# Where the 32 gate columns of the input projection are multiplied: from a fifth product of the first stage to a tail on the moving operand of the first value projection

## The chip, the core and the metric

The kernel runs on one core of a Trainium2 chip, as one program. The metric is the device time of one execution in microseconds (us); lower is better. The core's engines are named as in the profile: PE is TensorE's matrix multiplier, PEld its weight load (the stationary operand, which overlaps the multiplications), DVE is VectorE, ACT is ScalarE, POOL is GpSimd and SP is SyncE, which here only issues transfers. Each engine works through its own list of instructions in a fixed order; semaphores join the lists.

## What is computed

One layer of a decoder: a normalized input is projected to many groups of columns, two kinds of attention run on them, and an output projection and a SwiGLU feed-forward follow. For 512 tokens and a model width of 2048, the part that matters here is the combined input projection:

```python
h = _rms_norm(x, attn_norm[l])
proj = h @ w_in
qf, kf, vf, ff, qn, kc, vc, ks, vs, kw, vw, gt = jnp.split(proj, cuts, axis=-1)
log_f = jax.nn.log_sigmoid(ff + fox_forget_bias)         # 8 columns: forget gates
cum_f = jnp.transpose(jnp.cumsum(log_f, axis=1), (0, 2, 1))
gates = jax.nn.sigmoid(gt).reshape(B, T, G, R, 3)        # 24 columns: branch gates
```

`ff` (8 columns) and `gt` (24 columns) are the 32 gate columns. `kc` and `vc` (256 columns each) feed the compressed branch, `vs` and `vw` are values of the selected and of the window branch, two heads of 128 columns each, `ks`, `kw` and `qn` are keys and queries. The gates are first needed when the first attention head scales its probabilities, and the cumulative forget gate much later.

## The kernel before

**Precision.** All products are formed from operands split in two parts: `hi`, the value rounded to the fast format by an ACT copy, and `lo`, the rest, by a DVE subtraction. A product takes three matmuls: hi·hi, hi·lo and lo·hi (`mm3`, lines 170 to 173).

**First stage (lines 654 to 684).** A loop over the 16 blocks `k` of 128 input columns loads a block of x (`xs`, 256 KB) and of the weights of kc and vc (`ws`, 256 KB), splits x times its norm gain into `bigm` (kept for the whole attention part as the list `xg`) and the weights into `w0p`, and accumulates four products `first[0..3]`, one 128-column group each, all 512 tokens as moving operand. The row norm of x is not applied yet; squares of x are summed in `acc` on the side, and `rstd`, the reciprocal root, is multiplied in afterwards. `first[4]` is the fifth product: the 32 gate columns. Their weights `wf` (hi and lo side by side, 64 columns for each `k`) are stationary, and the hi and the lo part of x move through: two matmuls for each `k`, lines 675 to 677, into one PSUM bank of tag "o". The weights arrive in one transfer of 256 KB (`ws_fg`) at `k == 0` and are split by one ACT and one DVE instruction (lines 670, 671).

**Buffers.** `w0p`, `wf` and later all split projection weights are tiles of the tag "wp", of which there are two; raw weights are tiles "ws" (three) or "ox" (sixteen). A tile has to be released by its last reader before the next user of its slot can write. PSUM has eight banks, by tags: "g" two, "s" two, "t" two, "o" one, "m" one.

**After the first stage.** `ks0` is projected with the weights stationary (48 matmuls of 512 columns, lines 171 to 173), the row norm is finished meanwhile (`row_rstd`), and `unload` evicts `first[0..3]` times `rstd` as `t_kc` and `t_vc` (line 312) and `first[4]` as `fg` (line 698). It also transposes `rstd` into `rcol`, one column for each block of 128 tokens (line 703). Then `values(("vs0", "vw0"))` projects the values of both branches for the first head with the **tokens stationary**: for each chunk `c` of four `k`, each half `b` of the tokens, each `kk`, each block `t` of 128 tokens, three matmuls whose moving operand is 256 weight columns. Two banks "g" hold the four token blocks, two blocks each. The evictions (line 377 through `split2`) multiply by `rcol`.

**The gates.** `gates` (line 554) transposes `fg` back to tokens on partitions with four matmuls (line 558), adds the hi and lo halves to `tf`, and goes on to the branch gates `gate` and the cumulative sum (`lf`, `lfr`, a triangular product `ps_cum`).

**Order.** The program text interleaves a main list of steps with a side list (`weave`); after that a scheduler orders each engine's list before the run, so what stands where on an engine follows from its estimate of what is ready. The main list here is `values`, then the projections kw0, qn0 and qn1; the side list is the rest of `unload`, then `windows` and `compress` of kc (matmuls `z_kc`), `gates`, and the same for vc.

Of the kernel before, what the change touches and what calls it, by code (L numbers as in the profile page):

```python
# [17 lines left out]
P = 128  # L18
# [52 lines left out]
def hybrid_layer(ctx: ExitStack, tc: tile.TileContext, xT, vec, ffb, wfg, wfirst, win, cmpw, wout, wgu, wdn, out):  # L71
# [55 lines left out]
    def ftile(name):  # L127
        return pers.tile([P, T], F32, tag="f", name=name, bufs=4)
# [12 lines left out]
    def cut(m, at, n):  # L141
        return m[:, at:at + n]
# [11 lines left out]
    def parts_tile(name):  # L154
        return wpl.tile([P, 2 * HALF * P + P], FR, tag="wp", name=name, bufs=2)
# [138 lines left out]
    def gain(i):  # L294
        return gains[:, i:i + 1]
# [4 lines left out]
    rows = ap_.tile([P, 64], FR, name="rows")  # L300
    nc.vector.tensor_tensor(rows, rowsf, rowsf[:, 31:32].to_broadcast([P, 64]), op=OP.add)
    rcol = ap_.tile([P, NB], F32, name="rcol")


    nproj = [0]
# [46 lines left out]
        split2(r, t)  # L352
        live[name] = r

    def values(pair):

        z = [ps.tile([P, T], F32, tag="g", name=f"ps_{pair[0]}{b}", bufs=2) for b in range(2)]
        i = nproj[0]
        nproj[0] += 2
        for c in range(4):  # L360
            wp = load_w(win[i + c // 2, c % 2], f"{pair[0]}_{c}", 1 if c else 2)
            for b in range(2):
                for kk in range(4):
                    x = xg[4 * c + kk]
                    ws = slice(kk * 2 * HD, (kk + 1) * 2 * HD)
                    for t in range(2):
                        at = slice((2 * b + t) * P, (2 * b + t + 1) * P)
                        for n, (xp, w) in enumerate(((0, 0), (0, 1), (1, 0))):
                            nc.tensor.matmul(z[b][:, t * 2 * HD:(t + 1) * 2 * HD], x[:, xp, at], wp[w][:, ws],  # L369
                                             start=(c == 0 and kk == 0 and t == 0 and n == 0),  # L370
                                             stop=(c == 3 and kk == 3 and n == 2), skip_group_check=True)
                    yield
                if c == 3:
                    r = ap_.tile([P, 2, T], FR, tag="kv", name=f"{pair[0]}{b}", bufs=5)
                    for t in range(2):
                        ts = slice(t * 2 * HD, (t + 1) * 2 * HD)
                        split2([r[:, p, ts] for p in range(2)], z[b][:, ts], rcol[:, 2 * b + t:2 * b + t + 1])
                    live[pair[0], b] = r
        for n, name in enumerate(pair):
            def part(p, j, n=n, r=[live[pair[0], b] for b in range(2)]):  # L380
                return cut(r[j // 2][:, p], (2 * (j % 2) + n) * HD, HD)
            live[name] = part
# [170 lines left out]

    def gates():

        tp = ps.tile([P, NB, 64], F32, tag="t", name="ps_fgT", bufs=2)
        for i in range(NB):
            nc.tensor.transpose(tp[:, i, :], tokens["fg"][:64, i * P:(i + 1) * P], ident[:64, :64])
        yield
        tf = ftile("tf")[:, :NB * 32].rearrange("p (i c) -> p i c", c=32)  # L560
        nc.scalar.activation(tf, tp[:, :, :32], AF.Copy)
        nc.vector.tensor_tensor(tf, tf, tp[:, :, 32:], op=OP.add)
# [87 lines left out]
    for _ in range(WARM):  # L650
# [1 line left out]


    first = [ps.tile([P, T], F32, tag=tag, name=f"ps_first{i}", bufs=n)
             for i, (tag, n) in enumerate((("s", 2), ("s", 2), ("t", 2), ("t", 2), ("o", 1)))]
    for k in range(NK):
        xs = oxp.tile([P, T], F32, tag="ox", name=f"x_{k}", bufs=16)
        nc.sync.dma_start(xs, xT[k])
        ws = oxp.tile([P, T], F32, tag="ox", name=f"w0_{k}", bufs=16)
        nc.sync.dma_start(ws, wfirst[k])  # L660
        t = big(k)
        split(t, xs, v1(V_AN + k))
        wp = parts_tile(f"w0p_{k}")[:, :2 * T].rearrange("p (s c) -> p s c", s=2)
        w_done = split(wp, ws)
        if k == 0:
            wst = wpl.tile([P, HALF * P], F32, tag="ws", name="ws_fg", bufs=3)[:, :NK * 32]
            nc.sync.dma_start(wst, wfg)
            wst = wst.rearrange("p (k c) -> p k c", c=32)
            wf = parts_tile("wf")[:, :NK * 64].rearrange("p (k s c) -> p k s c", k=NK, s=2)
            nc.scalar.activation(wf[:, :, 0], wst, AF.Copy)  # L670
            nc.vector.tensor_tensor(wf[:, :, 1], wst, wf[:, :, 0].bitcast(F32), op=OP.subtract)
        for j in range(4):
            c = slice(j * P, (j + 1) * P)
            mm3(first[j], wp[:, 0, c], wp[:, 1, c], t[:, 0], t[:, 1], k == 0, k == NK - 1)
        for hl in range(2):
            nc.tensor.matmul(first[4][:64], wf[:, k], t[:, hl], start=(k == 0 and hl == 0),
                             stop=(k == NK - 1 and hl == 1))
        if k == 0:
            tc.add_manual_dep(nc.scalar.activation(acc, xs, AF.Square).ins, w_done.ins.name, PACE)
        else:  # L680
            sq = ftile(f"sq{k}")
            nc.scalar.activation(sq, xs, AF.Square)
            nc.vector.tensor_tensor(acc, acc, sq, op=OP.add)
        xg.append(t)


    ks0 = normed("ks0", gain(V_SK), "kv", 5)
    next(ks0)
    row_rstd("r1")

    def unload():
        for j, which in enumerate(("kc", "vc")):
            tokens[which] = []
            for g in range(2):
                tokens[which].append(scaled(first[2 * j + g], f"{which}{g}", True))
                yield
        fg = oxp.tile([P, T], F32, tag="ox", name="fg", bufs=16)
        nc.vector.tensor_tensor(fg[:64], first[4][:64], rstd[:64], op=OP.mult)
        tokens["fg"] = fg
        yield  # L700
        tr = ps.tile([P, NB, NH], F32, tag="t", name="ps_rT", bufs=2)
        for i in range(NB):
            nc.tensor.transpose(tr[:, i, :], rstd[:NH, i * P:(i + 1) * P], ident[:NH, :NH])
        nc.vector.tensor_copy(rcol, tr[:, :, 0])
        yield
# [1 line left out]
    N, NS, F, FS = 18, 26, 53, 12  # L707
    tokens_out = unload()
    weave(ks0, itertools.islice(tokens_out, 2), N, 2, 11)
    weave(stagger(values(("vs0", "vw0")), normed("kw0", gain(V_WK), "kv"), nsa_q(0), nsa_q(1)),  # L710
          chain(tokens_out, windows("kc", V_PK), compress("kc"), gates(), windows("vc", V_PV), compress("vc")), 5 * NK, 52, 10)
    def qf(h):
        return normed(f"qf{h}", gain(V_FQ), "q", 2)

# [602 lines left out]
```

## Time and profile before

| | |
|---|---|
| time, median of 3 runs (lowest to highest) | 2114.24 us (2113.95 to 2114.70) |
| the profiled execution: its time, its span | 2114.38 us, 2112.6 us |
| granted TensorE clock, mean | 1.00 |
| matmuls / DVE / ACT instructions in the span | 15675 / 2458 / 1242 |
| first stage, first to last matmul | 5.88 to 57.63 us of the span |
| `ks0` projection | 57.63 to 68.98 us |
| values of vs0 and vw0 | 68.98 to 96.18 us |

The span runs from the first to the last instruction of the profiled execution, and 1.8 us of its time lie around it. In a view of groups, a row has the line, the engine, the operation, the tile written and the tiles read, the shapes, the count, and then the busy time. In a timeline the first two columns are the start and the duration in us, and brackets at the end give the idle time of the engine before this row and what ended it. In a view of windows the columns are the length of the window and then, for each engine, the busy time with the count of instructions, the granted clock, the share of the DMA engines and GB/s. Durations of matmuls overlap (one is still draining when the next has begun), so the cost of one is the distance from start to start, not its duration.

### The profile page before, as it was taken

What the parts mean: (1) busy time and instruction counts of PE and PEld (TensorE: products, weight loads), DVE (VectorE), ACT (ScalarE), POOL (GpSimd) and SP (SyncE); (2) the same over time, 40 slices, a digit from 0 to 9 for tenths busy, and PEclk for the clock granted to TensorE, in tenths of its full rate; (3) what the DMA queues carried; (4) which work ended last, traced back from release to release, by engine and by line L of the source; (5) the groups of instructions that cost most, each with busy time, mean ns of one, the idle gap of its engine ahead of it and who ended that gap; (6) DMA issues with size and microseconds to landing.
All of it is one profiled execution on the core that took longest, in us unless ns stands there. A gap on an engine that the chain in (4) does not pass through costs nothing.

```text
span 2112.6 us, 37997 instructions
## 1 busy us (share of the span) xinstructions
PE 2101.6 (99%) x15675; PEld 1974.6 (93%) x15675; DVE 1675.4 (79%) x2458; ACT 999.7 (47%) x1242; POOL 190.7 (9%) x283
## 2 busy tenths in 40 slices
PE   9999999999999999999999999999999999999999
PEld 7878988888988888999999999999999999999999
DVE  6667667554567454999999999899999987889898
ACT  5555555444455343544334343343343455565554
POOL 0000000111211000111111111111111000000000
PEclk9999999999999999999999999999999999999999
DMA  5422111222222444676776777777787798579865
GB/s 196 160 75 62 61 58 58 65 86 85 90 85 75 152 137 137 170 188 202 193 195 189 193 197 182 201 187 184 205 191 195 225 335 270 151 233 329 302 174 149
DMA packets 113486, 349.63 MB, mean 165 GB/s; under 512 B 13592, under 2 KB 13592, under 8 KB 113312
## 3 DMA queue, kind: packets, MB, share of 16 engines
q1 hardware_dynamic: 85552, 270.33, 39.5%
q0 software_dynamic: 22144, 52.44, 14.0%
q10 hardware_dynamic: 5616, 24.43, 2.9%
q8 instruction: 122, 2.00, 0.4%
q14 instruction: 52, 0.43, 0.1%
HBM read 318.56 MB, written 74.73 MB: 186 GB/s over the span
## 4 chain that ended last, share of the span: by engine, by line
PE 85%; issue 9%; DVE 3%; POOL 1%; ACT 1%; DMA 0%; POOLq 0%; SPq 0%; ACTq 0%; DVEq 0%
PE q L1067 39%; PE pd L1206 13%; PE pd L1211 6%; PE po L172 3%; PE po L173 3%; PE po L171 3%; PE ps_vs L369 2%; PE ps_vf L369 1%; PE ps_qn L171 1%; PE ps_qn L173 1%; PE ps_qn L172 1%; POOL nbf L628 1%; PE ps_first L171 1%; PE ps_first L173 1%; PE ps_first L172 1%
## 5 line engine op out<-in xcount | busy, mean ns | idle before, releaser
L82 ACT ACTIVATE bigm<-r 128x1792 fp32r<-128x1792 f32 x174 | 298.2, 1714 | 461.1 <-PE q L1067 263.4
L79 DVE TENSOR_TENSOR bigm<-r,bigm 128x1792 fp32r<-128x1792 f32 x174 | 351.5, 2020 | 13.2 <-ACT bigm L82 12.7
L79 DVE TENSOR_TENSOR r<-r 128x512 f32<-128x512 f32 x522 | 267.2, 512 | 27.5 <-DMA r<-wgu 15.2
L1067 PE MATMUL q<-bigm 128*128 128x256 f32 x1848 | 217.5, 276 | 0.2 <-ACT bigm L82 0.2
L1067 PE MATMUL q<-formy,bigm 128*128 128x256 f32 x1848 | 217.1, 276 | 0.0
L1067 PE MATMUL q<-forma,bigm 128*128 128x256 f32 x1848 | 216.8, 276 | 0.0
L1067 PE MATMUL q<-formx,bigm 128*128 128x256 f32 x1848 | 216.8, 276 | 0.0
L1067 PEld LDWEIGHTS q<-bigm 128*128 128x128 f32 x1848 | 213.3, 188 | 0.6 <-ACT bigm L82 0.4
L1067 PEld LDWEIGHTS q<-formy,bigm 128*128 128x128 f32 x1848 | 213.1, 188 | 0.1
L1067 PEld LDWEIGHTS q<-forma,bigm 128*128 128x128 f32 x1848 | 213.0, 188 | 0.1
L1067 PEld LDWEIGHTS q<-formx,bigm 128*128 128x128 f32 x1848 | 212.9, 188 | 0.0
L124 POOL DMA_DIRECT2D wsum<-wdn x176 | 119.8, 687 | 878.7 <-ACT bigm L82 773.7
L1206 PE MATMUL pd<-bigm 128*128 128x256 f32 x1200 | 146.9, 276 | 0.0
L1206 PEld LDWEIGHTS pd<-bigm 128*128 128x128 f32 x1200 | 141.0, 188 | 0.0
L79 DVE TENSOR_TENSOR bigm<-wd,bigm 128x1024 fp32r<-128x1024 f32 (+1 forms) x62 | 107.8, 1739 | 12.3 <-ACT bigm L82 12.2
L82 ACT ACTIVATE bigm<-rawm 128x768 fp32r<-128x768 f32 (+2 forms) x72 | 66.0, 927 | 98.2 <-PE pd L1211 63.8
L369 PE MATMUL ps_vf<-wp_vf,bigm 128*128 128x256 f32 x768 | 101.7, 282 | 0.0
L171 PE MATMUL po<-bigm,wp_o 128*128 128x512 f32 x256 | 99.7, 389 | 0.0
L172 PE MATMUL po<-bigm,wp_o 128*128 128x512 f32 x256 | 99.7, 389 | 0.0
L173 PE MATMUL po<-bigm,wp_o 128*128 128x512 f32 x256 | 99.6, 389 | 0.0
L369 PEld LDWEIGHTS ps_vf<-wp_vf,bigm 128*128 128x128 f32 x768 | 95.1, 189 | 1.5 <-issue 0.7
L82 ACT ACTIVATE bigm<-wd 128x1024 fp32r<-128x1024 f32 (+1 forms) x62 | 91.1, 1469 | 10.7 <-DVE wd L79 6.1
(479 smaller groups left out, 3975.8 us busy)
## 6 DMA issues: line engine op xcount, KB each, us to landing
r<-wgu SPq DMA_DIRECT2D x174, 512.0 KB, 4.3
wsum<-wdn POOLq DMA_DIRECT2D x176, 256.0 KB, 5.1
rawm<-ad SPq DMA_DIRECT2D x44, 512.0 KB, 6.9
wd<-wdn SPq DMA_DIRECT2D x40, 512.0 KB, 6.0
wd<-wsum SPq DMA_DIRECT2D x40, 512.0 KB, 7.0
ad<-cb ACTq DMA_DIRECT2D x22, 896.0 KB, 6.0
rawm<-ad SPq DMA_DIRECT2D x44, 384.0 KB, 3.8
ws_o<-wout SPq DMA_DIRECT2D x28, 512.0 KB, 3.6
```

The costliest lines, as they stand in the source:

```text
L79: return pin(nc.vector.tensor_tensor(*args, op=op))
L82: return pin(nc.scalar.activation(*args, **kw))
L124: d = nc.gpsimd.dma_start(step[0], step[1], **step[2])
L171: nc.tensor.matmul(o, lh, rh, start=start, stop=False)
L172: nc.tensor.matmul(o, lh, rl, start=False, stop=False)
L173: nc.tensor.matmul(o, ll, rh, start=False, stop=stop)
L369: nc.tensor.matmul(z[b][:, t * 2 * HD:(t + 1) * 2 * HD], x[:, xp, at], wp[w][:, ws], start=(c == 0 and kk == 0 and t == 0 and n == 0), sto ...
L628: nc.gpsimd.tensor_scalar(nb[:, :n], ck[:, :n], ncq[:, i, h:h + 1], 1.0, op0=OP.add, op1=OP.mult)
L1067: nc.tensor.matmul(o, w[wp][:, fb, cs], a[:, xp, fa], start=(k == 0 and h == 0 and wp == 0 and xp == 0), stop=(g == NG - 1 and kk == 1 and ...
L1206: nc.tensor.matmul(b[q][k][:, h * 256:(h + 1) * 256], w[0][:, fb, q * P:(q + 1) * P], a[xp][:, fa], start=(j == 0 and h == 0 and xp == 0), ...
L1211: nc.tensor.matmul(b[q][k][:, h * 256:(h + 1) * 256], w[1][:, fb, q * P:(q + 1) * P], a[0][:, fa], start=False, stop=(j == NJ - 1), skip_g ...
```

## The change

The fifth product of the first stage goes, with its bank, its weight tile `wf`, the load `ws_fg` at `k == 0`, the split of the weights, the eviction `fg` and the four transposes in `gates`. The same 256 KB of gate weights are loaded once after the first stage as `gcols`. `values(("vs0", "vw0"), gcols)` appends them to the moving operand: the hi tile of a chunk has for each `k` 256 value columns, 32 gate columns hi and 32 gate columns lo. The three matmuls of a token block become x hi times 320 columns, x hi times 256 columns (the lo part of the value weights, now in two tiles of the sixteen "ox" buffers), and x lo times 288 columns. A block of 128 tokens now fills 320 columns, so each has a bank of its own: "g", "o", "s", "g". At the end one ACT and one DVE instruction for each block put the gate columns, times `rcol`, into `tf`. All other value projections are as before; the side list has two steps fewer, so its stated length falls from 52 to 50.

```diff
-    def values(pair):
+    def values(pair, gcols=None):
...
+            z = [ps.tile([P, T], F32, tag=tag, name=f"ps_{pair[0]}{t}", bufs=n)
+                 for t, (tag, n) in enumerate((("g", 2), ("o", 1), ("s", 2), ("g", 2)))]
...
+                st = wpl.tile([P, HALF * P], F32, tag="ws", name=f"ws_{name}", bufs=3)
+                load(st, w)
+                st = st.rearrange("p (k c) -> p k c", k=4)
+                hi = cut(parts_tile(f"wp_{name}"), VOFF, 4 * 320).rearrange("p (k c) -> p k c", k=4)
+                nc.scalar.activation(hi[:, :, :256], st, AF.Copy)
+                g = gcols[:, 4 * c:4 * c + 4]
+                nc.scalar.activation(hi[:, :, 256:288], g, AF.Copy)
+                lo = []
+                for n in range(2):
+                    t = loose(f"wl_{name}{n}").rearrange("p (k c) -> p k c", k=2)
+                    nc.vector.tensor_tensor(t, st[:, 2 * n:2 * n + 2], hi[:, 2 * n:2 * n + 2, :256].bitcast(F32), op=OP.subtract)
+                    lo += [t[:, kk] for kk in range(2)]
+                nc.vector.tensor_tensor(hi[:, :, 288:320], g, hi[:, :, 256:288].bitcast(F32), op=OP.subtract)
+                wp = [[hi[:, kk, :320] for kk in range(4)], lo, [hi[:, kk, :288] for kk in range(4)]]
+                cols = [320, 256, 288]
...
-                        for n, (xp, w) in enumerate(((0, 0), (0, 1), (1, 0))):
-                            nc.tensor.matmul(z[b][:, t * 2 * HD:(t + 1) * 2 * HD], x[:, xp, at], wp[w][:, ws],
+                        for n, xp in enumerate((0, 0, 1)):
+                            nc.tensor.matmul(z[2 * b + t][:, :cols[n]], x[:, xp, at], wp[n][kk],
...
+        if gcols is not None:
+            for t in range(NB):
+                rc = rcol[:, t:t + 1]
+                nc.scalar.activation(tf[:, t], z[t][:, 288:320], AF.Copy, scale=rc)
+                nc.vector.scalar_tensor_tensor(tf[:, t], z[t][:, 256:288], rc, tf[:, t], op0=OP.mult, op1=OP.add)
...
     def gates():
-        tp = ps.tile([P, NB, 64], F32, tag="t", name="ps_fgT", bufs=2)
-        for i in range(NB):
-            nc.tensor.transpose(tp[:, i, :], tokens["fg"][:64, i * P:(i + 1) * P], ident[:64, :64])
-        yield
-        tf = ftile("tf")[:, :NB * 32].rearrange("p (i c) -> p i c", c=32)
-        nc.scalar.activation(tf, tp[:, :, :32], AF.Copy)
-        nc.vector.tensor_tensor(tf, tf, tp[:, :, 32:], op=OP.add)
...
-             for i, (tag, n) in enumerate((("s", 2), ("s", 2), ("t", 2), ("t", 2), ("o", 1)))]
+             for i, (tag, n) in enumerate((("s", 2), ("s", 2), ("t", 2), ("t", 2)))]
...
-        if k == 0:
-            wst = wpl.tile([P, HALF * P], F32, tag="ws", name="ws_fg", bufs=3)[:, :NK * 32]
-            nc.sync.dma_start(wst, wfg)
-            wst = wst.rearrange("p (k c) -> p k c", c=32)
-            wf = parts_tile("wf")[:, :NK * 64].rearrange("p (k s c) -> p k s c", k=NK, s=2)
-            nc.scalar.activation(wf[:, :, 0], wst, AF.Copy)
-            nc.vector.tensor_tensor(wf[:, :, 1], wst, wf[:, :, 0].bitcast(F32), op=OP.subtract)
...
-        for hl in range(2):
-            nc.tensor.matmul(first[4][:64], wf[:, k], t[:, hl], start=(k == 0 and hl == 0),
-                             stop=(k == NK - 1 and hl == 1))
...
+    gcols = oxp.tile([P, T], F32, tag="ox", name="gcols", bufs=16).rearrange("p (k c) -> p k c", c=32)
+    nc.sync.dma_start(gcols.rearrange("p k c -> p (k c)"), wfg)
...
-        fg = oxp.tile([P, T], F32, tag="ox", name="fg", bufs=16)
-        nc.vector.tensor_tensor(fg[:64], first[4][:64], rstd[:64], op=OP.mult)
...
-    weave(stagger(values(("vs0", "vw0")), normed("kw0", gain(V_WK), "kv"), nsa_q(0), nsa_q(1)),
-          chain(tokens_out, windows("kc", V_PK), compress("kc"), gates(), windows("vc", V_PV), compress("vc")), 5 * NK, 52, 10)
+    weave(stagger(values(("vs0", "vw0"), gcols), normed("kw0", gain(V_WK), "kv"), nsa_q(0), nsa_q(1)),
+          chain(tokens_out, windows("kc", V_PK), compress("kc"), gates(), windows("vc", V_PV), compress("vc")), 5 * NK, 50, 10)
```

More of the change, by code (lines that the diff above doesn't have):

```diff
@@ L302, in hybrid_layer @@
     rcol = ap_.tile([P, NB], F32, name="rcol")
+    tf = ap_.tile([P, NB, 32], F32, name="tf")
     nproj = [0]
@@ L353, in normed @@
         live[name] = r
-    def values(pair):
-        z = [ps.tile([P, T], F32, tag="g", name=f"ps_{pair[0]}{b}", bufs=2) for b in range(2)]
+    def values(pair, gcols=None):
+        if gcols is None:
+            z = [ps.tile([P, T], F32, tag="g", name=f"ps_{pair[0]}{b}", bufs=2) for b in range(2)]
+            z = [z[t // 2][:, t % 2 * 2 * HD:(t % 2 + 1) * 2 * HD] for t in range(NB)]
+        else:
+            z = [ps.tile([P, T], F32, tag=tag, name=f"ps_{pair[0]}{t}", bufs=n)
+                 for t, (tag, n) in enumerate((("g", 2), ("o", 1), ("s", 2), ("g", 2)))]
         i = nproj[0]
@@ L360, in values @@
         for c in range(4):
-            wp = load_w(win[i + c // 2, c % 2], f"{pair[0]}_{c}", 1 if c else 2)
+            name = f"{pair[0]}_{c}"
+            w = win[i + c // 2, c % 2]
+            if gcols is None:
+                wp = [[x[:, kk * 2 * HD:(kk + 1) * 2 * HD] for kk in range(4)] for x in load_w(w, name, 1 if c else 2)]
+                wp.append(wp[0])
+                cols = [2 * HD] * 3
+            else:
+                st = wpl.tile([P, HALF * P], F32, tag="ws", name=f"ws_{name}", bufs=3)
[13 more added lines that the diff above has]
+                cols = [320, 256, 288]
             for b in range(2):
@@ L364, in values @@
                     x = xg[4 * c + kk]
-                    ws = slice(kk * 2 * HD, (kk + 1) * 2 * HD)
                     for t in range(2):
                         at = slice((2 * b + t) * P, (2 * b + t + 1) * P)
-                        for n, (xp, w) in enumerate(((0, 0), (0, 1), (1, 0))):
-                            nc.tensor.matmul(z[b][:, t * 2 * HD:(t + 1) * 2 * HD], x[:, xp, at], wp[w][:, ws],
-                                             start=(c == 0 and kk == 0 and t == 0 and n == 0),
+                        for n, xp in enumerate((0, 0, 1)):
+                            nc.tensor.matmul(z[2 * b + t][:, :cols[n]], x[:, xp, at], wp[n][kk],
+                                             start=(c == 0 and kk == 0 and n == 0 and (t == 0 or gcols is not None)),
                                              stop=(c == 3 and kk == 3 and n == 2), skip_group_check=True)
@@ L376, in values @@
                         ts = slice(t * 2 * HD, (t + 1) * 2 * HD)
-                        split2([r[:, p, ts] for p in range(2)], z[b][:, ts], rcol[:, 2 * b + t:2 * b + t + 1])
+                        split2([r[:, p, ts] for p in range(2)], z[2 * b + t][:, :2 * HD], rcol[:, 2 * b + t:2 * b + t + 1])
                     live[pair[0], b] = r
+        if gcols is not None:
[3 more added lines that the diff above has]
+                nc.vector.scalar_tensor_tensor(tf[:, t], z[t][:, 256:288], rc, tf[:, t], op0=OP.mult, op1=OP.add)
         for n, name in enumerate(pair):
@@ L696, in unload @@
                 yield
-        fg = oxp.tile([P, T], F32, tag="ox", name="fg", bufs=16)
-        nc.vector.tensor_tensor(fg[:64], first[4][:64], rstd[:64], op=OP.mult)
-        tokens["fg"] = fg
-        yield
         tr = ps.tile([P, NB, NH], F32, tag="t", name="ps_rT", bufs=2)
```

## The prediction

> **What bounds the kernel now.** I read the busy times and the chain of waits first.
>
> ```profile
> PE 2101.6 (99%) x15675; PEld 1974.6 (93%) x15675; DVE 1675.4 (79%) x2458; ACT 999.7 (47%) x1242; POOL 190.7 (9%) x283
> PE 85%; issue 9%; DVE 3%; POOL 1%; ACT 1%; DMA 0%; POOLq 0%; SPq 0%; ACTq 0%; DVEq 0%
> ```
>
> PE is busy from end to end, so time is gained or lost where PE's own list grows or shrinks, or where PE waits. Next I cut the stages that the change touches into windows: all engines, then the matmuls into `ps_first` alone, before and after the last gate matmul, and DVE's load while x is being split.
>
> ```profile
> 5.88:57.63 51.75, 51.75 (x225) 39.96 (x225) 33.02 (x55) 29.67 (x51) 0.83 (x1) 1.00 0.49 178
> 57.63:68.98 11.35, 11.35 (x51) 9.38 (x50) 9.16 (x11) 6.01 (x9) 0.00 (x0) 1.00 0.45 140
> 68.98:96.18 27.20, 26.14 (x218) 25.50 (x216) 14.08 (x23) 13.15 (x22) 0.00 (x0) 1.00 0.70 232
> ...
> 5.88:33.10 27.22, 27.22 (x116) 19.69 (x117) 0.00 (x0) 1.00 0.93 337
> 33.10:57.63 24.53, 24.53 (x109) 20.08 (x107) 0.00 (x0) 1.00 0.00 1
> ...
> 5.25:33.10 27.85, 27.50 (x117) 19.69 (x117) 26.42 (x46) 24.13 (x43) 0.83 (x1) 1.00 0.93 337
> ```
>
> The first stage has no PE idle time. The second part holds 108 matmuls (the 109th starts the next stage): 24.53/108 = 227 ns each, for 512 columns. The first part, where DVE is 95% busy and the gate matmuls run, takes 27.22/116 = 235 ns each. The granted clock is 1.00 throughout.
>
> **Removed from the first stage.** These rows show the gate matmuls, and how ACT's writes of `w0p` wait for PE.
>
> ```profile
> L676 PE MATMUL ps_first<-bigm,wf x32: 387/390/398, 8.7 to 32.9; 128*64 128x512 f32 x32
> ...
> 6.12 0.64 ACT L670 ACTIVATE wf<-ws_fg 128x512 fp32r<-128x512 f32 x1 [0.30 <-DMA ws_fg<-wfg]
> 16.77 0.63 ACT L82 ACTIVATE w0p<-w 128x512 fp32r<-128x512 f32 x1 [0.38 <-PE ps_first L173]
> 36.07 0.63 ACT L82 ACTIVATE w0p<-w 128x512 fp32r<-128x512 f32 x1 [2.13 <-PE ps_first L173]
> ```
>
> The stage keeps 192 matmuls. If the 84 early ones keep 235 ns and 108 have 227 ns, it lasts 44.2 us, 7.5 less; if all have 227 ns, 43.6 us, 8.15 less. There is one trap. While `wf` holds one of the two "wp" slots, `w0p` has the other alone: ACT may write block k only when PE has finished block k-1 (16.77), and the four or five gate matmuls, about 1.1 us, are what PE does during that 0.63 us copy. They look like filler. But the slot leaves with them. After the last gate matmul both slots serve `w0p`: ACT waits 2.13 us for PE (36.07), is a block ahead, and PE has no gap. In the changed kernel's order ACT writes the second `w0p` directly after the second x, and the load of `wfg`, third in SP's queue, is replaced there by x, so each early load lands one place earlier. DVE is the tight one; its three steps for a block follow each other here:
>
> ```profile
> 13.89 0.69 DVE L79 TENSOR_TENSOR w0p<-w,w0p 128x512 fp32r<-128x512 f32 x1
> 14.50 0.69 DVE L683 TENSOR_TENSOR acc<-acc,sq 128x512 f32<-128x512 f32 x1
> 15.10 0.74 DVE L138 SCALAR_TENSOR_TENSOR bigm<-x,vt,bigm 128x512 fp32r<-128x512 f32 x1
> 15.76 0.69 DVE L683 TENSOR_TENSOR acc<-acc,sq 128x512 f32<-128x512 f32 x1
> ```
>
> From start to start they take 0.61, 0.60 and 0.66 us. Its new order puts all sixteen splits of x and sums and eleven `w0p` first: 16 x 1.26 + 11 x 0.61 = 26.9 us from 5.25, done at 32.2 with nothing idle; PE asks for the eleventh `w0p` at its 123rd matmul, 5.88 + 122 x 0.23 = 33.9. So DVE keeps ahead by a microsecond or so, and small steps in between take part of it. I take **-7.7**, bounds -8.15 and -6.0 (1.5 us lost to DVE).
>
> **Removed with the transposes.** Four transposes, and a slow re-entry of the next matmul.
>
> ```profile
> 109.44 0.41 PE L558 MATMUL ps_fgT<-ident,fg 64*128 64x64 f32 x4
> 109.78 0.50 PE L171 MATMUL ps_kw<-bigm,wp_kw 128*128 128x512 f32 x1
> 110.11 0.40 PE L172 MATMUL ps_kw<-bigm,wp_kw 128*128 128x512 f32 x1
> ```
>
> 109.78 - 109.44 = 0.34 us. The re-entry (0.33 instead of 0.23) probably stays with the transpose `zkT` ahead of it. **-0.35**, bounds -0.45 and -0.3.
>
> **Added columns.** Of the 192 value matmuls, 64 grow by 64 and 64 by 32 columns. The trace has no such lengths; the nearest rows are a window of 256-column matmuls and the value matmuls themselves.
>
> ```profile
> 1000.00:1100.00 100.00, 100.00 (x885) 1.00 0.73 188
> ...
> 73.59 7.77 PE L369 MATMUL ps_vs<-wp_vs,bigm 128*128 128x256 f32 x66
> 81.29 0.41 PE L703 MATMUL ps_rT<-ident,rstd 8*128 8x8 f32 x4
> ```
>
> 100/885 = 113 ns for 256 columns, 227 for 512: (227 - 113)/256 = 0.446 ns a column, so 64 x (64 + 32) x 0.446 = **+2.74**. In place the 66 value matmuls take 7.70/66 = 117 ns, so 192 of them carry 0.7 us over the dense pace. Longer matmuls may absorb that (low bound +2.0); the lo part at another place in memory, and the 320-column stride, may double it, and a bit (high bound +4.0). I stay with 2.74.
>
> The Trainium skill (TensorE: Matmul & The Clock Gate, Back-to-back issue gap) gives columns/2.4 + 2.5 ns when warm: 109 and 216 ns, where the rows have 113 and 227. By its slope the added columns would be an estimated 2.56 us instead of 2.74; the rows decide.
>
> **The wait in front of `ss_ks`.** The only PE wait of this stage, and the ACT and DVE rows that lead to it:
>
> ```profile
> 72.53 0.50 PE L259 MATMUL ss_ks<-fr_ks,ones 128*128 128x512 f32 x1 [1.01 <-ACT fr_ks L82]
> ...
> 69.15 1.19 ACT L472 ACTIVATE xb_kc<-qq 128x480 fp32r<-128x480 f32 x2 [2.07 <-DVE qq L473]
> 70.25 1.05 ACT L82 ACTIVATE wp_vs<-ws_vs 128x1024 fp32r<-128x1024 f32 x1
> 71.20 0.61 ACT L334 ACTIVATE sq_ks<-t_ks 128x512 f32<-128x512 f32 x1
> 71.84 0.63 ACT L82 ACTIVATE fr_ks<-sq_ks 128x512 fp32r<-128x512 f32 x1
> ...
> 64.77 2.12 DVE L312 TENSOR_TENSOR t_vc<-ps_first,rstd 128x512 f32<-128x512 f32 x2
> 67.87 0.67 DVE L698 TENSOR_TENSOR fg<-ps_first,rstd 64x512 f32<-64x512 f32 x1
> 69.83 0.67 DVE L314 TENSOR_TENSOR t_ks<-ps_ks,rstd 128x512 f32<-128x512 f32 x1
> ```
>
> ACT idled 2.07 us for DVE, which was evicting `t_vc` (2.12). In the new order `t_vc` stands behind `fr_ks`, and `fg` is gone. On the old clock `t_ks` can then start at about 69.2, the second weight copy when its slot is free (69.1, 1.05 us), the square at 70.2, a small gate copy, `fr_ks` hi at 71.0 to 71.5. PE reaches `ss_ks` after 19 matmuls, six triples of 142 + 113 + 127 ns and one more: 68.98 + 2.44 = 71.4. About 0.2 us are left of 1.01: **-0.8**, bounds -1.1 and 0.
>
> **Preparation, evictions, loads: hidden.**
>
> ```profile
> L82 ACT ACTIVATE vs<-ps_vs,rcol x8: 456/474/477, 92.3 to 267.3; 128x256 fp32r<-128x256 f32 x8
> L151 DVE SCALAR_TENSOR_TENSOR vs<-ps_vs,rcol,vs x8: 455/479/483, 92.8 to 268.4; 128x256 fp32r<-128x256 f32 x8
> L561 ACT ACTIVATE tf<-ps_fgT x1: 278/278/278, 109.9 to 109.9; 128x128 f32<-128x128 f32 x1
> L562 DVE TENSOR_TENSOR tf<-tf,ps_fgT x1: 286/286/286, 110.2 to 110.2; 128x128 f32<-128x128 f32 x1
> 66.73 1.22 DVE L79 TENSOR_TENSOR wp_vs<-ws_vs,wp_vs 128x1024 fp32r<-128x1024 f32 x1
> 85.98 0.40 PE L489 MATMUL z_kc<-wp_kc,qq 128*128 128x256 f32 x2
> 96.18 0.39 PE L171 MATMUL ps_kw<-bigm,wp_kw 128*128 128x512 f32 x1
> ```
>
> A chunk's split grows from two to five instructions: one more on ACT (under 0.28 us, the 128-wide row) and on DVE two halves of 0.69 and a small one for one of 1.22, some 0.45 us more. The first was ready 1.0 us before PE's 68.98; with `t_vc` out of its way it is ready earlier still. The `tf` reads are eight instructions of under 0.29 us. The one PE could wait for is block 0's: its bank goes to `kw0` next. Blocks 0 and 1 end 24 matmuls (3 us) and three `z_kc` pairs before `kw0`, the two copies, two `wp_kc` splits and two `tf` reads ahead of that take about 3.0 us, so it is covered with under 1 us to spare; uncovered, it would cost up to 2. On SP, `gcols` stands behind the last load of x, far from its use. Two weight loads have moved ahead of the first `kc` loads, and the second waits for the raw tile of chunk 1, free at about 71.4 of the old clock; `z_kc` starts at 85.98, late enough. In `gates`, `zkT` now stands after the triangle's first matmul, and DVE writes that triangle between the small steps of `zks`: some 0.2 us. With 0.3 for DVE in the first stage: **+0.5**, bounds 0 and 1.5. Behind 150 us the instructions stand in the old order on every engine, so what is gained by then stays.
>
> **Sum.** -7.7 - 0.35 + 2.74 - 0.8 + 0.5 = -5.6. The profiled execution took 2114.38 (span 2112.6), the median of the runs is 0.14 less: 2114.38 - 5.6 - 0.14 = **2108.6 us**.
>
> **Rivals.**
> *The filler was needed.* Should `w0p` keep one slot for the first eight blocks, PE would stand still for each copy instead of doing gate matmuls, the 7.7 are not gained, and the added columns stay: 2114.24 - 0.35 + 2.74 = 2116.6, slower. The price decides against the change once the gaps exceed the forecast's 5.6 us over the seven blocks, 0.8 each. For it: 16.77. Against it: 36.07 and the new order.
> *DVE becomes the bound of the first stage.* At 95% busy, and with PE now asking every 2.73 us instead of 3.9, PE could wait 0.5 us at each of six blocks: 3 us, 2111.6. For it: the 26.42 of 27.85 us. Against it: a removed 0.69 us split, and DVE's second half of the stage nearly empty.
> *A new wait in the values:* `kw0` behind block 0's `tf`, or a late chunk: +2 us, 2110.6. For it: under 1 us to spare.
> *Alternating banks slow PE.* The four blocks are now written in turn to separate banks. Should the granted clock fall to half for the values, 24 us of matmuls double: about 2132. Against it: the first stage changes its bank among five all the time and its rows show clock 1.00.
> The Trainium skill (TensorE: Matmul & The Clock Gate, A second HAM failure mode: psum-queue depth-cycling) describes a kernel that cycled PSUM banks, idled briefly between groups and oscillated between the two clocks; the trace here disagrees, with 1.00 in that stage.
>
> **How the numbers follow.** Forecast 0.72; DVE bound 0.10; new wait 0.10; filler 0.06; banks 0.02. The forecast's own terms, all at their low bounds, give 2106.5, and all at their high bounds 2112; the first two rivals that follow lie inside. The range is 2106.4 to 2112.0. A measurement of this kernel can tell 0.2%, 4.2 us: below 2110.0 is faster. The forecast reaches over that in one case of ten (0.07); DVE's bound (0.10) and half of the new wait (0.05) lie within 0.2%, the other half below; filler and banks are slower: faster 0.70, same 0.22, slower 0.08.
>
> **What would show it.** The last `ps_first` matmul some 7.7 us earlier and no ACT, DVE or DMA named before `ps_first` matmuls; value triples of 383 ns; the `ss_ks` wait under 0.4 us; no idle time before the first `ps_kw`; the order and pace unchanged behind 150 us. Idle time in front of `ps_first`, or a value pace far over 383 ns a triple, would prove it wrong.

## The result, and the profile after

The changed kernel takes 2111.25 us (median of 20 runs, 2110.48 to 2111.92), the kernel before 2114.48 in the same comparison (20 runs, 2113.74 to 2115.24): a ratio of 0.9984, 95% interval 0.9979 to 0.9990, so some 3.2 us less. The forecast was 5.6 less, 2108.6 us; the time lies inside the range, but 2.65 us above the forecast.

The page of the changed kernel says the same of the bound as before, its busy times and its chain of waits:

```profile
PE 2095.5 (99%) x15639; PEld 1973.3 (94%) x15639; DVE 1674.8 (79%) x2467; ACT 1000.0 (47%) x1248; POOL 191.8 (9%) x283
PE 86%; issue 9%; DVE 2%; POOL 1%; ACT 1%; DMA 0%; POOLq 0%; SPq 0%; ACTq 0%; DVEq 0%
```

PE has 36 matmuls less, the 32 of the gates and the four transposes. To see where the time went, the span is cut at the first matmuls of the stages, the same ones in both kernels. The windows of the changed kernel (columns: start and end, length, then busy time and instructions of PE, PE's weight loads, DVE, ACT, POOL; granted clock, DMA share, GB/s; the fourth stretch of the table is left out) are: first stage; the `ks` projection; the values up to the first `ps_kw`; the attention and the output projection; the first 336 matmuls of the feed-forward stage; the rest.

```profile
5.88:49.56 43.68, 43.68 (x192) 36.15 (x193) 31.89 (x54) 28.24 (x50) 2.04 (x1) 1.00 0.56 207
49.56:60.91 11.35, 11.35 (x51) 9.38 (x50) 8.01 (x13) 7.25 (x12) 0.00 (x0) 1.00 0.38 114
60.91:89.96 29.05, 29.05 (x218) 28.36 (x217) 17.25 (x31) 13.91 (x27) 0.00 (x0) 1.00 0.59 196
...
167.92:841.09 673.17, 670.32 (x3693) 575.35 (x3691) 401.57 (x796) 324.40 (x579) 50.32 (x70) 1.00 0.27 88
...
841.09:884.23 43.14, 40.01 (x337) 39.13 (x336) 35.97 (x51) 20.22 (x20) 5.48 (x8) 1.00 0.60 162
...
884.23:2108.90 1224.67, 1220.04 (x10758) 1219.84 (x10756) 1124.00 (x1399) 558.86 (x468) 129.17 (x191) 1.00 0.73 212
```

The windows of the kernel before for the last three (its first three stand in the prediction: 51.75, 11.35 and 27.20):

```profile
174.76:847.88 673.12, 670.31 (x3692) 575.31 (x3691) 400.60 (x796) 324.50 (x579) 50.22 (x70) 1.00 0.28 89
...
847.88:887.84 39.96, 39.76 (x338) 39.23 (x336) 36.98 (x52) 20.22 (x20) 5.55 (x9) 1.00 0.64 168
...
887.84:2112.50 1224.66, 1220.03 (x10758) 1219.83 (x10756) 1124.50 (x1399) 558.22 (x468) 129.16 (x191) 1.00 0.75 212
```

| stretch | before | after | difference |
|---|---|---|---|
| first stage | 51.75 | 43.68 | -8.07 |
| `ks` projection | 11.35 | 11.35 | 0 |
| values, to the first `ps_kw` | 27.20 | 29.05 | +1.85 |
| from there to 174.76 (before) and 167.92 (after) | 78.58 | 77.96 | -0.62 |
| attention and output projection | 673.12 | 673.17 | +0.05 |
| first 336 matmuls of the feed-forward stage | 39.96 | 43.14 | **+3.18** |
| the rest | 1224.66 | 1224.67 | 0 |

The sum is -3.61, the difference of the spans (2109.0 and 2112.6). So the change as such brought 6.84 us up to 170 us, more than the forecast's 5.6, and PE kept them for 670 us. Then, in one place, 3.2 were given back. The timeline of the changed kernel there:

```profile
841.09 5.11 PE L1080 MATMUL q<-forma,bigm 128*128 128x256 f32 x42
841.28 0.33 SPq L85 DMA_DIRECT2D cb<-wgu  x1
...
844.99 1.61 DVE L79 TENSOR_TENSOR cb<-cb 128x512 f32<-128x512 f32 x3 [4.45 <-DMA cb<-wgu]
...
846.68 1.70 ACT L82 ACTIVATE bigm<-cb 128x1792 fp32r<-128x1792 f32 x1 [8.55 <-DVE cb L79]
...
848.43 5.15 PE L1080 MATMUL q<-formx,bigm 128*128 128x256 f32 x42 [2.24 <-ACT bigm L82]
```

And of the kernel before:

```profile
839.55 0.33 SPq L85 DMA_DIRECT2D r<-wgu  x1
842.63 0.33 SPq L85 DMA_DIRECT2D cb<-wgu  x1
...
847.88 5.11 PE L1067 MATMUL q<-forma,bigm 128*128 128x256 f32 x42
```

`cb` takes the second block of weights of the feed-forward stage. Before, its load went out 5.25 us ahead of the first `q` matmul; after, 0.19 us behind it. It lands 3.6 us later, DVE makes three sums of it, ACT copies it, and PE, done with the first 42 matmuls, stands still for 2.24 us, and for 0.59 and 0.15 us in front of two later groups. The waits of SP's queue name the releaser (total, times, longest). In the changed kernel and in the one before:

```profile
SPq L85 <- PE po L173: 8.5, 1, 8.5
```

```profile
SPq L85 <- PE po L173: 2.7, 1, 2.7
```

In both kernels the load waits for PE's matmuls of the output projection. How long the row is says little, since it counts from when the queue comes to this load (in e5 below it reads 8.1 us, and the load is in time). What counts is which matmul releases it. The 5.25 us ahead of the first `q` matmul and the 0.19 us behind it lie 5.44 us apart, which is 24 matmuls of 227 ns, PE's work on one `wp_o` tile. So the load now waits for one `wp_o` tile more than before. Nothing of the change touches that load, and SP's list of instructions is the same there. What has changed is where things lie. When the output projection ends, the pool of the weight ring closes, and the feed-forward stage's tiles are laid into the same memory:

```python
    wst_.close()
    fpl = ctx.enter_context(tc.tile_pool(name="fpl", bufs=1, side="right", reuse_waits="tile"))
    ca = fpl.tile([P, 4, T], F32, name="ca")
    cb = fpl.tile([P, 4, T], F32, name="cb")
```

The addresses that the two programs give to these tiles when they are built (bytes in a partition), with what the slot held last:

| memory | before | after | laid over it |
|---|---|---|---|
| "wp" slot A, 199200 to 207904 | last `wp_o` | last but one | `ca` (200224 to 208416) |
| "wp" slot B, 207904 to 216608 | last but one | **last `wp_o`** | **`cb`** (208416 to 216608) |
| "ws" slots 2 and 3, 220704 to 228896 | last raw `ws_o` (slot 3) | last but one (slot 2) | `r0` |

With `wf` gone from the two slots, the later tiles of the ring come to lie one slot further, down to the last weights of the output projection. That was theory S: `cb` now lies over the last `wp_o`, so its load must wait for PE's last matmul of the projection. The rivals: the loads of the new stage can't come 6.8 us earlier whatever the slot (T), or something that the earlier order of work has moved.

### The profile page after: what moved, and what is told of

It is laid out like the page before. It is cut to its first block, busy times and chain, and to the rows that moved or that the text cites. A ratio compares the mean times of both kernels' runs of the same rounds, so it can differ in the third digit from the quotient of the medians.

```text
span 2109.0 us, 37948 instructions
## 1 busy us (share of the span) xinstructions
PE 2095.5 (99%) x15639; PEld 1973.3 (94%) x15639; DVE 1674.8 (79%) x2467; ACT 1000.0 (47%) x1248; POOL 191.8 (9%) x283
## 4 chain that ended last, share of the span: by engine, by line
PE 86%; issue 9%; DVE 2%; POOL 1%; ACT 1%; DMA 0%; POOLq 0%; SPq 0%; ACTq 0%; DVEq 0%
PE q L1080 39%; PE pd L1219 13%; PE pd L1224 6%; PE po L172 3%; PE po L173 3%; PE po L171 3%; PE ps_vs L396 2%; PE ps_vf L396 1%; PE ps_qn L171 1%; PE ps_qn L173 1%; PE ps_qn L172 1%; POOL nbf L653 1%; PE ps_first L171 1%; PE ps_first L173 1%; PE ps_first L172 1%
```

## The experiments

The times of the kernel before beside these runs were 2114.3 (e1 to e4), 2114.52 (e5 to e7) and 2114.43 us (e8, e9); ratios are to it.

**e1: the ring turned by one.** In front of the first stage:

```diff
+    shift = parts_tile("shift")
+    nc.gpsimd.memset(shift[:, :32].bitcast(F32), 0.0)
     for k in range(NK):
```

> The changed kernel with one more tile in the ring of two weight slots: before the first stage a tile of the "wp" ring is taken and 32 of its columns are set to zero by POOL, so the first w0p takes the other slot, and so does every tile behind it; the last wp_o lies where it lay before the change. Nothing else is changed. Theory S (the slot): the changed kernel is 6.8 us ahead up to the last output projection (828 us of the old trace) and gives 3.2 back at the start of the feed-forward stage, because the tile cb lies over the slot that now holds the last wp_o, so its load waits for PE's last po matmul. Then here the load of cb is issued about 5 us before the first q matmul again, the waits of 2.2 and 0.6 us in front of q are gone, and the time is 2111.25 - 3.2 = 2108.05 (2107.7 to 2108.5). Rival T (the loads of the feed-forward stage cannot come 6.8 us earlier, whatever slot cb has: queue, transfers, the ring of raw tiles that is also turned by one): the waits stay, 2111.2. Rival E (the turned order of the first splits costs the first stage something): between the two.

Measured: 2112.88 us, 0.9993 (0.9984 to 1.0002), far from 2108.05. The timeline of its start and its windows (first stage; first 336 matmuls of the feed-forward stage) show two things:

```profile
9.42 0.61 ACT L699 ACTIVATE sq<-x 128x512 f32<-128x512 f32 x1
...
9.94 1.13 ACT L82 ACTIVATE w0p<-w 128x512 fp32r<-128x512 f32 x2
...
10.61 0.79 PE L171 MATMUL ps_first<-bigm,w0p 128*128 128x512 f32 x1 [5.46 <-ACT w0p L82]
```

```profile
10.61:56.23 45.62, 45.62 (x192) 37.50 (x193) 29.50 (x45) 25.74 (x44) 0.21 (x1) 0.95 0.46 159
847.64:886.58 38.94, 38.94 (x337) 38.87 (x336) 35.50 (x51) 20.36 (x21) 5.49 (x8) 1.00 0.62 168
```

The added tile had moved the first `w0p` behind four splits of x and a square on ACT; PE stood still for 5.46 us and then ran at a lower granted clock (0.95 over the stage), so the first stage ended at 56.23 instead of 49.56. But the feed-forward stage's first 336 matmuls took 38.94 instead of 43.14 us, with no wait: 4.2 us less, against an expected 3.2. The slot theory held at its place; the repair had spoilt another one. Rival E, a cost in the first stage, had been given at most the 3.2 us that S gains; at 6.67 us it was larger than the gain.

**e2: `ca` and `cb` exchanged in the kernel before.**

```diff
-    ca = fpl.tile([P, 4, T], F32, name="ca")
     cb = fpl.tile([P, 4, T], F32, name="cb")
+    ca = fpl.tile([P, 4, T], F32, name="ca")
```

> The kernel before with the allocations of ca and cb in the other order, so that cb lies over the slot that holds the last wp_o and ca over the other; the first 600 us are untouched, and no work comes earlier or later up to there. Theory S: the load of cb is issued right behind PE's last po matmul (848 instead of 842.6 us), PE waits 2 to 3 us in front of the second group of q matmuls, and the time is 2114.48 + 3.2 = 2117.7 (2117.2 to 2118.2). Rival T (what was lost behind the change is lost because PE arrives 6.8 us earlier): PE arrives at its old time here, so 2114.5.

Measured: 2119.34 us, 1.0022 (1.0013 to 1.0031): 5.0 us slower, where S had 3.2 and T nothing. Its timeline, and the windows of the first 43 `q` matmuls, of the wait, of the 6.83 us after it and of the rest:

```profile
848.21 0.33 SPq L85 DMA_DIRECT2D cb<-wgu  x1
```

```profile
856.79 5.38 PE L1067 MATMUL q<-formx,bigm 128*128 128x256 f32 x24 [3.66 <-ACT bigm L82]
```

```profile
848.02:852.85 4.83, 4.83 (x43) 4.83 (x41) 0.94 (x1) 0.00 (x0) 0.00 (x0) 1.00 0.73 222
852.85:856.79 3.94, 0.28 (x4) 0.08 (x2) 2.16 (x5) 1.75 (x2) 0.00 (x0) 0.78 0.89 360
856.79:863.62 6.83, 6.83 (x38) 6.83 (x39) 6.31 (x8) 4.21 (x4) 1.09 (x2) 0.63 0.21 57
863.62:893.03 29.41, 29.41 (x258) 29.34 (x257) 27.48 (x40) 14.28 (x16) 4.40 (x6) 1.00 0.62 149
```

Nothing of the change is in this kernel, and PE reached the stage at its old time (848.02). `cb` laid over the last `wp_o` is enough to produce the wait: rival T falls. The wait is longer here, 3.66 us: DVE's first sum of `cb` starts at 853.3, 5.1 us behind the load, where the changed kernel has 3.7; why the data came later was not followed. A clock loss comes on top: 38 matmuls in 6.83 us are 180 ns each instead of 113, at a granted clock of 0.63. The Trainium skill (TensorE: Matmul & The Clock Gate, Why this matters for your kernels) warns of PE idle gaps of more than about 3 us inside a kernel, since the clock then drops to half. That agrees with these two kernels: 3.66 us cost clock, the 2.24 us of the changed kernel did not (its window has 1.00).

**e3: the kernel of e1 without the added columns.**

```diff
-                cols = [320, 256, 288]
+                cols = [256, 256, 256]
...
-                            nc.tensor.matmul(z[2 * b + t][:, :cols[n]], x[:, xp, at], wp[n][kk],
+                            nc.tensor.matmul(z[2 * b + t][:, :cols[n]], x[:, xp, at], wp[n][kk][:, :256],
...
```

> The kernel of e1 with the added columns left out: all 192 value matmuls read 256 columns, from the same weight tiles with their stride of 320 columns, into the four banks as in the changed kernel; the splits of the gate columns stay. tf is filled from value columns in place of the gates' columns, so the gates' projection is left out of the computation. Theory C (the added columns cost what they are long): 64 x 96 x 0.446 = 2.74 us less than e1, so 2105.3 if e1 is 2108.05, and value matmuls of 117 ns as before the change. Rival B (part of the price is the four banks, the stride or the lo parts in another tile): less than 2 us is gained, and the value matmuls stay above 117 ns: 2106.0 or more.

Measured: 2110.52 us, 0.9982 (0.9973 to 0.9991), 2.36 less than e1: between theory C's 2.74 and the 2 below which rival B would stand. Both kernels have the spoilt start, so e6 repeats it on clean ground.

**e4: a slot held through the first blocks.**

```diff
+        if k == 0:
+            held = parts_tile("held")
+            nc.gpsimd.memset(held[:, :32].bitcast(F32), 0.0)
+        if k == 12:
+            nc.gpsimd.tensor_tensor(tf[:, 0], held[:, :32].bitcast(F32), t[:, 1, :32].bitcast(F32), op=OP.add)
```

> The changed kernel with one slot of the weight ring held through the first blocks, as wf held it before the change, but without the gate matmuls: behind the first w0p a tile is taken, 32 columns are set to zero, and POOL reads them together with the lo part of the thirteenth x. Until then w0p_1 to w0p_5 have one slot, each behind the one before; the last wp_o comes to lie in the harmless slot, as in e1. Theory F (the gate matmuls were filler in front of each copy while wf held the slot, and the change takes the slot's hold and the filler away together): PE stands still for the hi copy of ACT and part of the lo of DVE at each of five blocks, 0.7 to 1.3 us each, 3.5 to 6.5 us in all: 2111.5 to 2114.5 where e1 is 2108.05. Rival D (DVE's lo parts set the pace of these blocks, not the slot): under 1 us more than e1, 2108 to 2109.

Measured: 2112.36 us, 0.9990 (0.9981 to 0.9999). It can't be compared with e1, whose start is spoilt; against e5 (below), which like this one has no PE wait at the start of the feed-forward stage, it is 5.2 us more. The group of `ps_first` matmuls that open a product (its idle time stands behind the bar):

```profile
L171 PE MATMUL ps_first<-bigm,w0p 128*128 128x512 f32 x64 | 25.5, 407 | 4.5 <-ACT w0p L82 4.2 <-ACT bigm L137 0.4
```

There are five waits of 4.2 us in all for ACT's `w0p`: 0.84 us a block, as theory F had it. A single slot without the gate matmuls stops PE at each of the five copies. The trap named in the prediction is there; the change avoids it only since the slot is given up with the matmuls.

**e5: `cb` laid elsewhere, the ring left alone.**

```diff
-    ca = fpl.tile([P, 4, T], F32, name="ca")
     cb = fpl.tile([P, 4, T], F32, name="cb")
+    ca = fpl.tile([P, 4 * T + P], F32, name="ca")[:, P:].rearrange("p (a t) -> p a t", a=4)
```

> The changed kernel with cb allocated ahead of ca and 512 bytes of slack below ca, so that cb lies wholly over the slot whose last wp_o is the one before the last; every engine's list of instructions is the one of the changed kernel, the first stage too. Theory S: the first 830 us are those of the changed kernel (6.8 us ahead of before at the last po matmul), the load of cb goes out some 5 us before PE's last po matmul, no PE wait is left in front of q (as in e1 and e4), the 3.2 us stay and 1.2 come on top, since r0 is loaded early as well: 2111.25 - 4.4 = 2106.9 (2106.4 to 2107.4). Rival (the waits in e1 and e4 were gone only because PE came 6 us later there): the waits come back, 2109.5 to 2111.3.

Measured: 2107.16 us, 0.9966 (0.9953 to 0.9978): faster than both kernels. Its load queue, and its windows (first stage, values, first 336 matmuls of the feed-forward stage):

```profile
828.13 0.33 SPq L85 DMA_DIRECT2D r<-wgu  x1
836.61 0.33 SPq L85 DMA_DIRECT2D cb<-wgu  x1
```

```profile
5.82:50.16 44.34, 44.34 (x193) 36.66 (x193) 32.10 (x54) 28.49 (x50) 0.83 (x1) 1.00 0.56 208
61.51:90.55 29.04, 29.04 (x217) 28.35 (x216) 17.21 (x31) 13.90 (x26) 0.00 (x0) 1.00 0.59 198
...
841.86:880.62 38.76, 38.76 (x337) 38.69 (x336) 35.33 (x51) 20.23 (x20) 5.48 (x8) 1.00 0.63 168
```

`cb` goes out 5.25 us before the first `q` matmul, as in the kernel before, and PE (841.86) comes as early as in the changed kernel, within 0.8 us. There is no wait: 38.76 us for the 336 matmuls, 4.38 less than the changed kernel. So PE's early arrival was not the cause, the slot was. Over all runs, where `cb` lies over the last `wp_o` its load goes out 0.19 us behind the first `q` matmul (the changed kernel, e2), and elsewhere 5.25 us ahead of it (the kernel before, e1, e4, e5).

**e6: e5 without the added columns** (the edit of e3).

> The kernel of e5 with the added columns left out: all value matmuls read 256 columns (e3's edit without the turned ring); the gates' projection is left out of the computation. Theory C: 2.74 us less than e5: 2104.2 if e5 is 2106.9, lead at the end of the values 2.7 us more. Rival B (banks, stride, lo parts in another tile cost some of it): less than 2 us of difference to e5.

Measured: 2104.21 us, 0.9952 (0.9939 to 0.9966): 2.95 less than e5, with 2.74 expected. Its windows, first stage and values:

```profile
5.99:49.68 43.69, 43.69 (x193) 36.14 (x193) 31.91 (x54) 28.22 (x50) 0.83 (x1) 1.00 0.56 208
61.03:87.36 26.33, 26.33 (x218) 25.81 (x216) 16.54 (x30) 13.26 (x25) 0.00 (x0) 1.00 0.58 202
```

29.04 - 26.33 = 2.71 us for the added columns. The windows are the better measure here, since the first stages of these two executions alone differ by 0.65 us (44.34 and 43.69). This kernel still has the four banks, the stride and the lo part in another tile; the kernel before needed 27.20 us for the same matmuls, 1.01 of them the wait for `fr_ks` and 26.19 without it. So these three cost some 0.15 us together.

**e7: `wf` out of the ring, the gate matmuls kept**, in the kernel before, with `cb` placed as in e5.

```diff
-            wf = parts_tile("wf")[:, :NK * 64].rearrange("p (k s c) -> p k s c", k=NK, s=2)
+            wfs = [oxp.tile([P, T], FR, tag="ox", name=f"wf{i}", bufs=16).rearrange("p (k s c) -> p k s c", k=8, s=2) for i in range(2)]
...
```

> The kernel before with the gates' weights wf in two tiles of the "ox" ring instead of a slot of the weight ring; the 32 gate matmuls stay, w0p has both slots from the start; cb is placed as in e5, because the ring is turned by this too. It tells the slot's part of the first stage's gain from the matmuls' part. Theory A (32 matmuls of 227 ns are 7.3 us, the rest of the 8.1 us is PE's loss to the single slot): the first stage ends 0.7 to 0.9 us earlier and the time is 2114.3 - 0.8 = 2113.5; at the start of the feed-forward stage it stands as before, since the raw tiles' ring is not turned here. Rival F (the slot costs nothing, the gate matmuls cover it): 2114.3.

Measured: 2115.97 us, 1.0009 (1.0000 to 1.0018), where both theories had 2114.3 or less; the interval only just allows for no change at all. Its windows of the first stage:

```profile
5.82:12.00 6.18, 5.67 (x21) 3.96 (x22) 4.47 (x13) 4.41 (x11) 0.31 (x1) 1.00 1.03 393
12.00:33.10 21.10, 21.10 (x94) 16.70 (x93) 21.10 (x35) 19.35 (x34) 0.00 (x0) 1.00 0.86 311
33.10:58.46 25.36, 25.36 (x112) 19.92 (x111) 7.18 (x10) 5.83 (x10) 0.00 (x0) 1.00 0.01 2
```

The stage takes 52.64 us instead of 51.75. From 12 us to 33.10 it is at the dense pace (94 matmuls in 21.10 us, 224 ns); ahead of that it has only 21 matmuls in 6.18 us, and there the waits name ACT's and DVE's splits of x in front of gate matmuls, which had come to stand ahead of an x that was not split yet. So the run tells nothing of the slot. What it alone cost in the kernel before stays unsettled: the stage's excess over the dense pace, 51.75 - 224 x 0.227 = 0.9 us, is its upper bound.

**e8 and e9: `r0` and `cc` exchanged**, in e5 and in the kernel before. An allocation of `r0`'s tag ahead of `cc` moves `r0` over the first two raw slots:

```diff
+    fpl.tile([P, 8, 256], F32, tag="r0", name="r0", bufs=1)
     cc = fpl.tile([P, 2, T], F32, name="cc")
```

> The kernel of e5 with the memory of r0 and cc exchanged: r0 now lies over the raw slot of the last ws_o. It asks whether the rest of e5's gain at the start of the feed-forward stage (7.2 us of lead behind it, 6.0 before it) comes from r0's load, which goes out once that slot's splits are done. Theory R: r0 is loaded 5.4 us later than in e5, as before the change, the small gaps among the first q matmuls come back, and the time is 2107.16 + 1.2 = 2108.4 (2107.9 to 2108.9). Rival: the gain has another cause, 2107.2.

> The kernel before, with the same exchange of r0 and cc: here it puts r0 over the raw slots of the two loads ahead of the last one. The mirror of e8, without anything of the change. Theory R: r0's load goes out 5.4 us earlier than in the kernel before (834 instead of 839.6 us), the gaps among the first q matmuls shrink by 1.2 us, and the time is 2114.4 - 1.2 = 2113.2 (2112.8 to 2113.6). Rival: 2114.4.

Measured: e8 2107.69 us, 0.9967 (0.9955 to 0.9980); e9 2113.64 us, 0.9996 (0.9987 to 1.0005). Both lie between theory R and its rival, just outside the range that R had given (2107.9 to 2108.9, and 2112.8 to 2113.6), and their intervals hold both; by the times alone the question would be open. The windows of the 336 matmuls are, first of e8, then of e9:

```profile
841.20:881.14 39.94, 39.50 (x338) 39.04 (x336) 36.68 (x52) 20.36 (x21) 5.50 (x8) 1.00 0.63 170
```

```profile
848.54:887.32 38.78, 38.78 (x338) 38.70 (x336) 35.34 (x51) 20.24 (x20) 5.49 (x8) 1.00 0.62 168
```

With `r0` late they take 39.94 (before the change: 39.96), with `r0` early 38.78 (e5: 38.76). So of the 4.38 us between the changed kernel and e5, the kernel before would have had 3.18; the other 1.2 belong to `r0`, whose raw slot the change happened to turn the lucky way (with `ws_fg` the ring of raw tiles lost a tile too), and which only shows when `cb` isn't late.

## Why the prediction was right, and where it was wrong

**First stage, -7.7 forecast: -8.07.** All 192 matmuls keep 227 ns, the bound of -8.15 nearly reached. DVE didn't become the bound, and no gap stands for copies: both slots serve `w0p` from the start. e4 shows what the filler rival would have cost, 0.84 us a block. The prediction's 0.8 was the price at which waits at seven blocks eat up the forecast's 5.6 us; 7 x 0.84 = 5.9 would have done so. How the 8.07 us divide between the 32 matmuls (32 x 0.227 = 7.3 us) and the freed slot is not shown.

**Added columns, +2.74: 2.71 by the windows of e6, 2.95 by the times.** The triples are not 383 ns, though. Starts of the lo products in the changed kernel, six in a row:

```profile
61.06 0.28 PE L396 MATMUL ps_vs<-wl_vs,bigm 128*128 128x256 f32 x1
...
63.04 0.28 PE L396 MATMUL ps_vs<-wl_vs,bigm 128*128 128x256 f32 x1
...
63.47 0.50 PE L259 MATMUL ss_ks<-fr_ks,ones 128*128 128x512 f32 x1
```

(63.04 - 61.06)/5 = 396 ns. The forecast had put the dense pace under its landmark; the overhead of the value matmuls in place (117 ns instead of 113) stays with the longer ones. The difference, which alone enters the sum, was right.

**The wait in front of `ss_ks`, -0.8.** No idle time stands in its row: 1.0 is gained. The values' stretch, forecast at 2.74 - 0.8 = +1.94, came out at +1.85.

**Transposes -0.35 and new waits +0.5.** Together +0.15 forecast, -0.62 measured behind the first `ps_kw`. None of the forecast's new waits came, neither for `kw0` behind `tf` nor in the first stage. Another did: `sc`, the scores of the compressed branch, waits 0.3 us for DVE's `tmp_qn`, which it did not in this stretch before. So beyond the transposes some 0.6 us more went, with the reordering or otherwise, and no run takes that apart.

**Banks.** The clock is 1.00 in the values' window, and by e6 the alternating banks, with the stride and the lo tile, cost some 0.15 us. PE had no idle time there, so what alternating banks do where PE pauses between groups is not shown here.

**Range and chances.** All terms at their high bounds add up to -6.0 - 0.3 + 4.0 + 0 + 1.5 = -0.8, which is 2113.4 us, and not the 2112 that the prediction gives; its range was narrower than its own terms. It had also given 0.70 to a time below 2110.0, and 2111.25 is above that.

**The step that failed** is the last sentence of the prediction's costs: "Behind 150 us the instructions stand in the old order on every engine, so what is gained by then stays." The order was the old one, and the pace too, up to 841 us. But the same order does not mean the same waits. The prediction had followed the slot of `wf` only as far as the first stage, where giving it up was a gain, and not to the end of the ring, where it decides which memory the last weights lie in and whose load waits for them. The sign that the prediction named for this, order and pace unchanged behind 150 us, failed at 841 us. By the ledger, 1.24 us more than forecast were gained up front and 3.18 were lost there; most of what remains of the 2.65 us is that the changed kernel's profiled execution took 2110.77 us, 0.48 less than its median. That the time still lies inside the range is in part luck: with the front only as good as forecast, it would have been 2111.25 + 1.24 = 2112.5 us, above the range. With `cb` moved, 2107.16 us, the change gives more than was forecast, though 1.2 us of that belong to the slot of `r0`.

## What to carry to other kernels

Taking a tile out of a ring shifts the later tiles to other slots; where a later pool reuses the ring's memory, a load hundreds of microseconds away can change what it waits for, with no instruction moved. So after a change to a ring, compare when the first loads behind the pool's end go out, and which tiles they lie over, not only the order (the rows of the releaser read alike here), and lay the tile that is needed first over the slot that falls free first. Repairing a stall with an extra instruction in a tight stage can cost more than the stall (e1); for moving the tile in memory no cost showed (e5).

## What the runs showed of the hardware

A long wait of PE had a second price here. In e2 the 336 matmuls take 45.01 us: 38.76 without any wait (e5), 3.66 of standing still, and 2.5 more because the 38 matmuls behind the wait take 180 instead of 113 ns at the lower granted clock. In e1 a wait of 5.46 us at the start, where the changed kernel has 0.71, moved the first stage's end by 56.23 - 49.56 = 6.67 us. The start differs too, between two executions whose first matmuls are the same: the first four `ps_first` matmuls of the changed kernel and of e5 span 1.21 and 1.86 us.

```profile
5.88 1.21 PE L171 MATMUL ps_first<-bigm,w0p 128*128 128x512 f32 x4 [0.71 <-ACT bigm L137]
```

```profile
5.82 1.86 PE L171 MATMUL ps_first<-bigm,w0p 128*128 128x512 f32 x4 [0.29 <-ACT bigm L137]
```

The Trainium skill (TensorE: Matmul & The Clock Gate, What's actually happening) says that the clock is decided in free-running windows of about 3.4 us, so that the matmul at which it rises varies from run to run. These rows agree with it, but the recorded granted clock, 1.00 in both, doesn't show the difference. In the profiled executions such differences also blur e8 and e9: the first stage ends 0.36 us earlier in e8 than in e5 (49.80 and 50.16) and 0.59 later in e9 than in the kernel before (58.22 and 57.63), each time against the effect that was looked for.
